# Interleaving two arrays: the first store as two DMAs of 8 KiB and 24 KiB rows

## The chip, the cores and the metric

The kernel runs on one core of a Trainium2 chip. The time is device time in microseconds (us) of one execution; several executions are compared by their median. The work is moved by the core's 16 DMA engines between the large memory (DRAM, where the inputs and the output lie) and the core's own memory of 128 partitions, and done by one computing engine, VectorE (DVE in the profile). DMAs are issued by two other engines: SyncE (SP) and ScalarE (ACT), each with a queue of its own.

## The reference

Two arrays of 32 x 256 x 1024 float32 values, x and y, are woven into one of twice the size: every even place of the result holds a value of x, every odd place one of y.

```python
result = np.zeros((batch, seq, dim * 2), dtype=np.float32)
result[..., 0::2] = x
result[..., 1::2] = y
```

Seen flat, the result is x[0], y[0], x[1], y[1] and so on. 33.5 MB of x and as much of y are read and 67.1 MB are written; there is no arithmetic.

## The kernel before, in words

The flat inputs are cut into 9 tiles. A tile has 128 rows, one for each partition, and the rows of a tile lie one behind the other in DRAM. Tiles 1 to 7 are W = 8192 values wide (rows of 32 KiB, 4 MiB for each of x and y), tile 0 and tile 8 have 4096 (rows of 16 KiB, 2 MiB). Two buffers each for x (`xt`), y (`yt`) and the woven output (`ot`) are used in turn.

A tile is woven in pieces of at most 4096 values per row: tile 0 is piece 0, tiles 1 to 7 give two pieces each (1 to 14), tile 8 is piece 15. A piece of 4096 columns of input makes 8192 columns of output, so each of the 16 stores moves 128 rows of 32 KiB, 4 MiB. Even pieces use the first output buffer, odd ones the second.

Three engines run in their own order, written out by hand:

- SP issues the loads (L52): x of tile 0, then x and y of tile 1, 2 and so on in turn. From tile 2 on it waits (L59, L62) until VectorE has woven the last piece of the tile two before, since the buffer is the same. y of tile 0 is issued by ACT instead. The first load of either queue is moved ahead of the program's opening.
- VectorE weaves a piece with two copies: L72 puts x at the even columns of the output buffer, L75 puts y at the odd ones. Ahead of them it waits for the loads (L68, L74) and, from piece 2 on, for the store that used the same output buffer before (L70).
- ACT waits until both copies of a piece are done (L78) and issues its store (L79).

A DMA adds 16 to its semaphore when it has landed. The stores of the even pieces count on one semaphore, those of the odd pieces on the other, and L70 waits for piece i until the semaphore of its parity has reached 16 times the number of earlier pieces of that parity: `16 * (i // 2)`. At the end ACT waits for all even stores (L83) and SP for all odd ones (L88), and the semaphores are set back.

Each DMA of 128 rows is spread over the 16 DMA engines, 8 rows to each.

Of the kernel before, what the change touches and what calls it, by code (L numbers as in the profile page):

```python
# [3 lines left out]


def _interleave(nc, x, y, out):
    P = 128
    W = 8192
    fp32 = mybir.dt.float32  # L10

    total = 1
    for s in x.shape:
        total *= s
    assert total % (P * W) == 0
    FIRST = 4096
    widths = [FIRST] + [W] * (total // (P * W) - 1) + [W - FIRST]
    n = len(widths)

    def flat(ap):  # L20
        return ap.rearrange("b s d -> (b s d)")

    fx, fy, fo = flat(x), flat(y), flat(out)
    at = [P * sum(widths[:k]) for k in range(n)]

    def rows(ap, k, scale=1):
        a, w = scale * at[k], scale * widths[k]
        return ap[a : a + P * w].rearrange("(p w) -> p w", p=P)

    xt = [nc.alloc_sbuf_tensor(f"xt{b}", [P, W], fp32).ap() for b in (0, 1)]  # L30
    yt = [nc.alloc_sbuf_tensor(f"yt{b}", [P, W], fp32).ap() for b in (0, 1)]
    ot = [nc.alloc_sbuf_tensor(f"ot{b}", [P, W], fp32).ap() for b in (0, 1)]

    xsem = [nc.alloc_semaphore(f"xsem{b}") for b in (0, 1)]
    ysem = [nc.alloc_semaphore(f"ysem{b}") for b in (0, 1)]
    woven = nc.alloc_semaphore("woven")

    pieces = []
    for k, w in enumerate(widths):
        step = w // 2 if w > W // 2 else w  # L40
        pieces += [(k, c, c + step) for c in range(0, w, step)]
    last = {}
    for i, (k, _, _) in enumerate(pieces):
        last[k] = i
    m = len(pieces)
    end = (m - 1) % 2
    osem = [None, None]
    for b in (1 - end, end):
        osem[b] = nc.alloc_semaphore(f"osem{b}")

    def load(eng, tile, ap, k, sem):
        return eng.dma_start(out=tile[:, : widths[k]], in_=rows(ap, k)).then_inc(sem, 16)  # L52

    load(nc.sync, xt[0], fx, 0, xsem[0])
    load(nc.scalar, yt[0], fy, 0, ysem[0])
    for k in range(1, n):
        b = k % 2
        if k >= 2:
            nc.sync.wait_ge(woven, 2 * last[k - 2] + 1)  # L59
        load(nc.sync, xt[b], fx, k, xsem[b])  # L60
        if k >= 2:
            nc.sync.wait_ge(woven, 2 * last[k - 2] + 2)  # L62
        load(nc.sync, yt[b], fy, k, ysem[b])

    for i, (k, a, e) in enumerate(pieces):
        b = k % 2
        if a == 0:
            nc.vector.wait_ge(xsem[b], 16 * (k // 2 + 1))  # L68
        if i >= 2:
            nc.vector.wait_ge(osem[i % 2], 16 * (i // 2))  # L70
        o = ot[i % 2][:, : 2 * (e - a)]
        nc.vector.tensor_copy(out=o[:, 0::2], in_=xt[b][:, a:e]).then_inc(woven, 1)  # L72
        if a == 0:
            nc.vector.wait_ge(ysem[b], 16 * (k // 2 + 1))  # L74
        nc.vector.tensor_copy(out=o[:, 1::2], in_=yt[b][:, a:e]).then_inc(woven, 1)  # L75

    for i, (k, a, e) in enumerate(pieces):
        nc.scalar.wait_ge(woven, 2 * i + 2)  # L78
        nc.scalar.dma_start(  # L79
            out=rows(fo, k, 2)[:, 2 * a : 2 * e], in_=ot[i % 2][:, : 2 * (e - a)]  # L80
        ).then_inc(osem[i % 2], 16)

    nc.scalar.wait_ge(osem[1 - end], 16 * (m // 2))  # L83
    used = sorted(s.num for s in [*xsem, *ysem, woven, osem[1 - end]])
    assert used == list(range(used[0], used[-1] + 1)), used
    nc.scalar.sem_clear(range(used[0], used[-1] + 1))
    turns = (m + 1) // 2
    nc.sync.nop(nofuse=True).wait_op(osem[end], 16 * turns, "sem-ge").then_inc(  # L88
        osem[end], -16 * turns
    )  # L90

def kernel(tc, x, y, out):
    nc = tc.nc
    tc.close()
    tc.compile()

    _interleave(nc, x, y, out)

    blocks = nc.main_func.blocks
    for engine in (mybir.EngineType.SP, mybir.EngineType.Activation):  # L100
        opening = blocks[0].instructions
        at, moved = next(
            (b, i)
            for b in blocks[1:]
            for i in b.instructions
            if i.engine == engine and i.opcode == "DMACopy"
        )
        assert not (moved.sync_info and moved.sync_info.on_wait)
        body = at.instructions
        body.remove(moved)  # L110
        gate = next(
            n
            for n, i in enumerate(opening)
            if i.engine == engine and i.opcode == "Drain"
        )
        opening.insert(gate, moved)
        at.instructions = body
        blocks[0].instructions = opening


# [1 line left out]
_INS = ['x', 'y']  # L122
_OUTS = [((32, 256, 2048), 'float32')]


# [23 lines left out]
```

## Time and profile before

| | us |
|---|---|
| three runs | 314.58, 315.33, 317.65 (median 315.33) |
| the profiled execution | 314.62 |
| its span, first to last instruction | 313.3 |
| VectorE busy | 72.6 (32 copies, 2.29 to 2.30 each) |
| VectorE waiting for stores at L72 | 159.4 (13 times) |
| VectorE waiting for y at L75 | 47.2 (8 times) |
| VectorE waiting for x at L72 | 20.7 (2 times) |

All times in the text count from the first instruction of the span unless it says otherwise. A line such as "L72 DVE COPY" names the line of the kernel, the engine and the operation. A DMA issue has two times: how long the issuing engine is held (0.33 to 0.43 us here for loads, 0.34 to 0.36 for stores) and how long it takes until the data has landed (29.1 us in the middle for a store, 43.7 for x and 60.9 for y of a full tile). The second contains the time in which the DMA stands in its queue behind others.

Some landings and issues of the first 90 us, from the trace:

| | issued | landed |
|---|---|---|
| x of tile 0, y of tile 0 | 0.00, 0.12 | 11.46, 13.30 |
| x of tile 1, y of tile 1 | 1.57, 1.95 | 25.16, 42.07 |
| x of tile 2, y of tile 2 | 13.81, 16.01 | 55.42, 74.76 |
| store 0 | 16.02 | 39.62 |
| store 1 | 44.42 | 67.50 |
| store 2 | 48.83 | 86.81 |

### The profile page before, as it was taken

What the parts mean: (1) busy time and instruction counts of PE and PEld (TensorE: products, weight loads), DVE (VectorE), ACT (ScalarE), POOL (GpSimd) and SP (SyncE); (2) the same over time, 40 slices, a digit from 0 to 9 for tenths busy, and PEclk for the clock granted to TensorE, in tenths of its full rate; (3) what the DMA queues carried; (4) which work ended last, traced back from release to release, by engine and by line L of the source; (5) the groups of instructions that cost most, each with busy time, mean ns of one, the idle gap of its engine ahead of it and who ended that gap; (6) DMA issues with size and microseconds to landing.
All of it is one profiled execution on the core that took longest, in us unless ns stands there. A gap on an engine that the chain in (4) does not pass through costs nothing.

```text
span 313.3 us, 114 instructions
## 1 busy us (share of the span) xinstructions
DVE 72.6 (23%) x32; POOL 0.2 (0%) x4
## 2 busy tenths in 40 slices
DVE  0502062022050220502205022040221402250320
POOL 0000000000000000000000000000000000000000
DMA  8999999999999999999999999999999999999998
GB/s 347 456 389 414 448 423 431 439 423 448 418 452 410 460 402 469 402 469 402 460 410 456 414 439 431 423 448 423 448 414 456 406 464 402 435 435 464 406 443 360
DMA packets 4896, 134.22 MB, mean 428 GB/s; under 512 B 544, under 2 KB 544, under 8 KB 544
## 3 DMA queue, kind: packets, MB, share of 16 engines
q10 hardware_dynamic: 2448, 69.21, 51.2%
q1 hardware_dynamic: 2448, 65.01, 48.6%
HBM read 67.11 MB, written 67.11 MB: 428 GB/s over the span
## 4 chain that ended last, share of the span: by engine, by line
DMA 73%; DVE 11%; another core or an unknown queue 10%; issue 0%; SPq 0%; DVEq 0%
DMA out_dram<-ot 61%; DMA yt<-in_y_dram 13%; DVE ot L75 6%; DVE ot L72 5%; SPq L52 0%; DVEq L70 0%
## 5 line engine op out<-in xcount | busy, mean ns | idle before, releaser
L72 DVE COPY ot<-xt 128x4096 f32<-128x4096 f32 x16 | 36.7, 2295 | 180.0 <-DMA out_dram<-ot 159.4
L75 DVE COPY ot<-yt 128x4096 f32<-128x4096 f32 x16 | 36.7, 2292 | 47.2 <-DMA yt<-in_y_dram 47.2
L133 POOL MEMSET const-bfloat16-1.0<- 128x1 bf16 x1 | 0.1, 101 | 0.0
L133 POOL MEMSET const-uint8-127<- 128x1 uint8 x1 | 0.1, 101 | 0.0
L133 POOL MEMSET const-float32-0.0<- 128x1 f32 x1 | 0.1, 98 | 0.2 <-issue 0.2
L133 POOL MEMSET const-float32-1.0<- 128x1 f32 x1 | 0.1, 98 | 0.0
## 6 DMA issues: line engine op xcount, KB each, us to landing
out_dram<-ot ACTq DMA_DIRECT2D x16, 4096.0 KB, 29.1
xt<-in_x_dram SPq DMA_DIRECT2D x7, 4096.0 KB, 43.7
yt<-in_y_dram SPq DMA_DIRECT2D x7, 4096.0 KB, 60.9
xt<-in_x_dram SPq DMA_DIRECT2D x2, 2048.0 KB, 25.2
yt<-in_y_dram ACTq DMA_DIRECT2D x1, 2048.0 KB, 13.2
yt<-in_y_dram SPq DMA_DIRECT2D x1, 2048.0 KB, 51.2
```

The costliest lines, as they stand in the source:

```text
L72: nc.vector.tensor_copy(out=o[:, 0::2], in_=xt[b][:, a:e]).then_inc(woven, 1)
L75: nc.vector.tensor_copy(out=o[:, 1::2], in_=yt[b][:, a:e]).then_inc(woven, 1)
L133: nc = _bacc.Bacc("TRN2", target_bir_lowering=False, num_devices=1)
```

## The change

The store of piece 0 is no longer one DMA but two, issued by ACT one behind the other. The first takes the first 2048 of the 8192 output columns of each row (128 rows of 8 KiB, 1 MiB), the second the other 6144 (128 rows of 24 KiB, 3 MiB). Both add 16 to the even semaphore, so every wait on that semaphore counts 16 more than before: piece 2 waits for 32, piece 4 for 48, and the closing wait for 144. The odd semaphore's numbers stay as they were. All other stores, all loads and all copies are unchanged.

```diff
+    def parts(i, w):
+        return [slice(0, w // 4), slice(w // 4, w)] if i == 0 else [slice(0, w)]
+
+    def stored(b, i):
+
+        return sum(16 * len(parts(j, W)) for j in range(b, i, 2))
...
         if i >= 2:
-            nc.vector.wait_ge(osem[i % 2], 16 * (i // 2))
+            nc.vector.wait_ge(osem[i % 2], stored(i % 2, i))
...
         nc.scalar.wait_ge(woven, 2 * i + 2)
-        nc.scalar.dma_start(
-            out=rows(fo, k, 2)[:, 2 * a : 2 * e], in_=ot[i % 2][:, : 2 * (e - a)]
-        ).then_inc(osem[i % 2], 16)
+        for c in parts(i, 2 * (e - a)):
+            nc.scalar.dma_start(
+                out=rows(fo, k, 2)[:, 2 * a : 2 * e][:, c], in_=ot[i % 2][:, c]
+            ).then_inc(osem[i % 2], 16)

-    nc.scalar.wait_ge(osem[1 - end], 16 * (m // 2))
+    nc.scalar.wait_ge(osem[1 - end], stored(1 - end, m))
...
-    turns = (m + 1) // 2
-    nc.sync.nop(nofuse=True).wait_op(osem[end], 16 * turns, "sem-ge").then_inc(
-        osem[end], -16 * turns
-    )
+    turns = stored(end, m)
+    nc.sync.nop(nofuse=True).wait_op(osem[end], turns, "sem-ge").then_inc(
+        osem[end], -turns
+    )
```

## The prediction

> **What bounds the kernel now.** I read the head of the page first, then the DMA busy time by stretches, then the chain and the waits. The kernel only moves data (section 3 of the page: 67.11 MB read, 67.11 MB written), so the first question is whether the 16 DMA engines ever rest. The page:
>
> ```profile
> span 313.3 us, 114 instructions
> ...
> DVE 72.6 (23%) x32; POOL 0.2 (0%) x4
> ...
> DMA  8999999999999999999999999999999999999998
> ...
> DMA packets 4896, 134.22 MB, mean 428 GB/s; under 512 B 544, under 2 KB 544, under 8 KB 544
> ...
> out_dram<-ot ACTq DMA_DIRECT2D x16, 4096.0 KB, 29.1
> ```
>
> The reader is to see that the only computing engine works 23% of the span while DMA is at 9 in all slices but the first and the last. Digits hide a per cent, so the second view is busy time by stretches (columns: stretch, its length, DVE, POOL, clock, DMA share, GB/s):
>
> ```profile
> 4.00:16.00 12.00, 4.50 (x2) 0.00 (x0) 1.00 1.01 434
> 16.00:44.00 28.00, 4.20 (x2) 0.00 (x0) 1.00 1.01 424
> 44.00:67.00 23.00, 4.79 (x3) 0.00 (x0) 1.00 1.01 435
> 67.00:106.00 39.00, 9.09 (x4) 0.00 (x0) 1.00 1.01 434
> 285.00:300.00 15.00, 4.59 (x2) 0.00 (x0) 1.00 1.01 437
> 300.00:312.00 12.00, 0.00 (x0) 0.00 (x0) 1.00 1.01 437
> ```
>
> From 4 to 67, the stretch that the change touches, and to the end, the share is 1.0: the engines are full, whether loads and stores alternate (67 to 106), loads run alone (part of 16 to 44) or a store runs alone (300 to 312). Now the chain:
>
> ```profile
> 1.95 40.12 DMA yt<-in_y_dram
> ...
> 44.42 23.08 DMA out_dram<-ot
> ...
> 297.53 2.30 DVE ot L75
> ```
>
> It looks as if the store of piece 1 (issued at 44.42) waits for y of tile 1 (landed at 42.07), and VectorE for stores (159.4 us in 13 waits by L79's view). But every DMA step of this chain is time in which the engines serve that transfer and its neighbour in turn; shortening a step only lengthens another.
>
> The trace's records of single packets give the unit. Each 32 KiB row is one packet of 1.213 us on one engine, each 16 KiB row 0.611 us, each semaphore packet 0.009 us. An engine has 8 rows of every DMA. Work of one engine: 14 loads and 16 stores of 32 KiB rows, 30 x 8 x 1.213 = 291.1; 4 loads of 16 KiB rows, 4 x 8 x 0.611 = 19.6; 34 semaphore packets, 0.3; together 311.0 us. The first packet starts at 1.02 and the last ends at 312.84, so 311.8 us hold 311.0 of work; 0.8 is the cold start (the first 16 KiB rows take up to 1.5 us). **So nothing in the order of transfers can win more than about 0.8 us, and a loss has to come from engines that rest or from rows that cost more.**
>
> **The change part by part.**
>
> *Bytes and rows.* Store 0, 8 x 1.213 = 9.70 us of each engine, becomes 8 rows of 8 KiB and 8 of 24 KiB. The trace has no stores of these sizes. The line through its two sizes (0.602 us per 16 KiB, 0.009 fixed) gives 0.310 and 0.912 us, together 1.222: +0.009 x 8 = +0.07, and one more semaphore packet +0.009. I take **+0.08 us**. Bounds: below, zero, since the same bytes move and 24 KiB lies between measured sizes; above, the instruction fetches in the same records, which are 8 KiB packets and took 0.474 to 0.549 us: 8 x (0.549 - 0.310) = +1.9 us for the small part. I stay by the line, as its rows are transfers of the same kind on the same queue, the fetches are not.
>
> *One more issue on ACT's queue.* L79 takes 0.34 us. It lies at 16.4, right behind the first, and ACT next has something to do when piece 1 is woven (44.4 before). Nothing; without that cover it would be 0.34.
>
> *What moves.* The packet records show how the engines share: where 16 KiB loads meet 32 KiB stores (268 to 276) each 4 us holds 1.22 us of loads and 2.79 of stores, so the two queues alternate row by row, whatever a row's size. A queue that sends smaller rows therefore gets less. Replay of one engine from 20.9 us, when store 0 sends its first row (issued 16.02): tile 1 still has 1 row of x and 8 of y to load.
> Before: store 0's 8 rows and 6 load rows alternate to 20.9 + 14 x 1.213 = 37.9 (landed 39.62); the last 3 rows of y run alone to 41.5 (landed 42.07). Then loads alone until store 1, issued 44.42, sends from about 48.7. Between 20.9 and 48.7 this makes 15 load rows.
> After: eight 8 KiB rows alternate with eight load rows, one 24 KiB row, and the ninth: 20.9 + 8 x 0.310 + 9 x 1.213 + 0.912 = 35.2. So **y of tile 1 lands near 35.8 rather than 42.07**, and store 1 is issued near 38.1 rather than 44.42. The other seven 24 KiB rows alternate with five more load rows to 20.9 + 2.48 + 8 x 0.912 + 14 x 1.213 = 47.7, so **store 0 lands near 49.3 rather than 39.62**. Store 1 is queued by then and starts after one or two load rows, near 49 to 50: 15 or 16 load rows since 20.9, where before there were 15. The hole that store 1 left in its queue (37.9 to 48.7) goes, but loads filled that hole, so its going wins no time.
>
> *The wait that grows.* VectorE's wait before piece 2 (L70) now asks for both halves of store 0: its copies begin near 49.3, not at 44.31. Behind it are piece 2's two copies, behind these the loads of tile 3 (issued 46.62 and 48.82, now near 51.6 and 53.9) and store 2 (48.83, now 53.9). Who is late? The load queue reaches tile 3 at 75.1, when y of tile 2 is through: 23 us of cover. Store 2 sends at 67.9, behind store 1: 14 us of cover, and it takes the place of store 1's rows at once. Both costs are zero here.
>
> *Steady state and end.* From store 1 on every row is as before, with the loads level or one row (1.2 us) further ahead of the stores. The slack of this state is 9.7 us: a store is issued at 77.11, the one in front of it lands at 86.81. At the end y of tile 8 lands at 297.50, store 15 is issued at 299.86 and sends at 302.7 to 303.2, just as store 14 runs out (last packet 303.16). Loads further ahead make this place safer, by up to about 1 us. The closing waits change only in the number for the even semaphore.
>
> Sum: +0.08 us on the profiled execution, 314.62 (its span 313.3 and 1.3 around it), so 314.7. The three runs have the median 315.33, 0.7 above that execution, lowest 314.58. On the median: 315.33 + 0.08 = **315.4 us**.
>
> **The rivals.**
>
> *A fixed price for the second DMA.* If the engines paused between two DMAs, the price would be what passes from a store's last packet to its landing: 38.0 to 39.62, 1.6 us. Then 315.33 + 1.6 = 316.9, still within 1%. Against it: store 15's packets follow store 14's with no gap, share 1.01. Chance 0.05.
> The Trainium skill, "DMA: Bandwidth & Descriptors", section "Anatomy of one DMA", fits a DMA as about 2.0 us fixed plus bytes over 436 GB/s (for the path through gpsimd, which this kernel doesn't use); by it, as an estimate, the second DMA costs 2.0 us, 317.3. The trace agrees with the slope (437 GB/s) but shows the fixed part beside other packets.
>
> *Rows of the new sizes are dear; slower.* Place: store 0's 256 rows. If 24 KiB is sent as three of 8 KiB and each costs what an instruction fetch cost, an engine spends 32 x 0.549 = 17.6 us instead of 9.7: +7.9, 323.2. It decides (1%, 3.15 us) from (9.70 + 3.15) / 32 = 0.40 us per 8 KiB. For it: no record of a 24 KiB row. Against: 16 KiB rows cost half of 32 KiB to within 1%, so a row of 8 KiB would have to leave the line by 0.09. Chance 0.06.
>
> *A hole at the end; slower.* If the stores came out ahead by n load rows instead, y of tile 8 would land about 1.8 n later (a 16 KiB and a 32 KiB row each) and store 15 find its queue empty, with half a microsecond of slack: n = 2 gives +3, 318.4. The replay gives the other sign. Chance 0.02.
>
> *Faster.* The 0.8 us of cold start is before the changed place. Below 1% in any case; 0.03 for what runs scatter (314.58 to 317.65).
>
> *The split doesn't act* (the two DMAs share the engines as one): the time is the same, 315.4; it is part of the forecast's share.
>
> **How the numbers follow.** Forecast 0.84; 1% (3.15 us) is about what a measurement of this kernel tells from no change. Within 1%: 0.84 + 0.05 = 0.89; slower: 0.06 + 0.02 = 0.08; faster 0.03. The range: below, 314.4, the lowest run less 0.2 for the slack at the end; above, 317.4, which takes in the +1.9 us bound of 8 KiB rows and the fixed price.
>
> **What would show it.** Packets 5040 (4896 + 128 + 16) with 134.22 MB; an issue more; y of tile 1 landing near 36, VectorE's copy of it there and then a wait for store 0 of some 11 us to near 49; store 1 issued near 38; from 67 on the old rhythm of 38.7 us per tile; DMA share 1.0 in 16 to 67. Wrong if: share below 1 in 16 to 67 (a pause or dear rows), y of tile 1 still near 42 (no row-by-row turns), or packets at the end with no store behind store 14.

## The result and the profile after

Over 22 runs of each the changed kernel took 314.63 us (median; 314.23 to 315.27), the kernel before 315.81 (314.42 to 318.88). The ratio of the averages (314.64 and 316.24) is 0.9949, 95% interval 0.9925 to 0.9973. That is half a per cent faster in the average and 0.4% in the median, where 315.4 and no change had been forecast. The lowest times hardly differ (314.23 and 314.42); what went away is the upper part of the scatter. In a later comparison the changed kernel was at 314.80 (314.23 to 315.15) against 315.55 (314.45 to 319.59), ratio 0.9972 (0.9948 to 0.9996). Slow runs, more than 1.5% above the fastest of the same kernel, count in the medians and spans given here but not in the ratios.

The profiled executions show nothing of this gain: 314.58 us after, 314.62 before. The page of the changed kernel, the lines that answer to those of before:

```profile
span 313.2 us, 115 instructions
...
DMA  9999999999999999999999999999999999999998
...
DMA packets 5040, 134.22 MB, mean 428 GB/s; under 512 B 560, under 2 KB 560, under 8 KB 560
...
out_dram<-ot ACTq DMA_DIRECT2D x15, 4096.0 KB, 32.7
...
out_dram<-ot ACTq DMA_DIRECT2D x1, 3072.0 KB, 33.9
...
out_dram<-ot ACTq DMA_DIRECT2D x1, 1024.0 KB, 17.2
```

The same bytes go in 144 more packets, the engines are as full as they were, and the stores wait longer in their queue (32.7 us from issue to landing, 29.1 before). The same by stretches (stretch, its length, DVE, POOL, clock, DMA share, GB/s):

```profile
4.00:16.00 12.00, 4.38 (x2) 0.00 (x0) 1.00 1.01 433
16.00:44.00 28.00, 4.70 (x3) 0.00 (x0) 1.00 1.01 421
44.00:67.00 23.00, 4.50 (x2) 0.00 (x0) 1.00 1.02 440
67.00:106.00 39.00, 9.09 (x4) 0.00 (x0) 1.00 1.00 433
285.00:300.00 15.00, 4.59 (x2) 0.00 (x0) 1.00 0.99 426
300.00:312.00 12.00, 0.00 (x0) 0.00 (x0) 1.00 1.01 437
```

The chain of the changed kernel's first 55 us no longer runs through y of tile 1 but through the second part of store 0, which VectorE now waits for:

```profile
16.54 33.91 DMA out_dram<-ot
...
50.47 2.30 DVE ot L79
```

So the order of the transfers changed as foreseen, and the profiled time did not. The gain has to be looked for in executions that neither profile shows. The question for the runs was what makes some executions of the kernel before longer than 314.6.

### The profile page after: what moved, and what is told of

Read it like the earlier page. It is cut to its first block, busy times and chain, and to the rows that moved or that the text cites. A ratio compares the mean times of both kernels' runs of the same rounds, so it can differ in the third digit from the quotient of the medians.

```text
span 313.2 us, 115 instructions
## 1 busy us (share of the span) xinstructions
DVE 72.7 (23%) x32; POOL 0.2 (0%) x4
## 4 chain that ended last, share of the span: by engine, by line
DMA 84%; DVE 11%; ACTq 0%; issue 0%
DMA out_dram<-ot 65%; DMA yt<-in_y_dram 15%; DVE ot L82 6%; DVE ot L79 5%; DMA xt<-in_x_dram 4%; ACTq L87 0%
## 6 DMA issues: line engine op xcount, KB each, us to landing
out_dram<-ot ACTq DMA_DIRECT2D x15, 4096.0 KB, 32.7
out_dram<-ot ACTq DMA_DIRECT2D x1, 1024.0 KB, 17.2
```

## The experiments

A view that turned out to carry the answer is worked out from the trace's landing records. Every DMA is counted by 16 increments, one for each engine that moved 8 of its rows. The **lag** of a DMA is the time of its last increment less the median of its 16. The Trainium skill, "DMA: Bandwidth & Descriptors", section "Why a DMA increments its semaphore by 16 and not by 1", says that only the full count means that all data has landed; the traces agree, since every wait here ends with the last of the 16.

### Where a long execution loses its time

First theories: "lead" (loads too little ahead of the stores, so that the end gets a hole) against "gap" (the stretch without stores, 38 to 48.7 us). Two more executions of the kernel before, unchanged:

> The kernel before, unchanged, profiled once more, to see an execution of it that took longer than the one shown (314.62; the median of 22 runs is 315.81, the highest 318.88). Theory 'lead' (the loads stand too little ahead of the stores, so that in some executions y of tile 8 lands late and store 15 finds store 14 already gone): a long execution shows engines at rest just before store 15, between about 300 and 305 us, and y of tile 8 landing later than 297.5. Rival 'gap' (the stretch in which store 1's queue is empty and loads run alone, 38 to 48.7 us, is at times slower): a long execution shows x and y of tile 2 and everything after them late by the same amount, already at 60 us, and no rest at the end. If this execution is near 314.6 it tells nothing.

> As before_a: the same kernel, another execution. Lead: any excess over 314.6 us stands as rest of the DMA engines ahead of store 15. Gap: any excess is there by 60 us.

Measured: 315.49 us (before_a) and 314.90 (before_b). Later two more were taken, before_c and before_d:

> The kernel before once more, to see an execution above 316.5 us if one comes. Theory: its excess is that of one DMA engine, which falls behind during store 0 (and perhaps further later), while the other 15 end near 312.6. Rival: all 16 engines end later together.

> As before_c: another execution of the kernel before; one engine behind from store 0 on with the others at 312.6, or, by the rival, all of them late.

Measured: 314.61 and 316.02. The longest of them at its end (same columns as above):

```profile
300.00:312.00 12.00, 0.00 (x0) 0.00 (x0) 1.00 1.01 437
312.00:314.00 2.00, 0.00 (x0) 0.00 (x0) 1.00 0.00 0
```

for the execution of 314.62, and for that of 316.02:

```profile
300.00:312.00 12.00, 1.28 (x1) 0.00 (x0) 1.00 1.01 437
312.00:314.00 2.00, 0.00 (x0) 0.00 (x0) 1.00 0.04 16
```

There is no hole before 312 (share 1.01, 437 GB/s in both). But after 312 the longer execution still has a share of 0.04. A packet counts where it starts, so this is one more row on one engine (1.213 of 16 x 2 us). The packet records say it outright: 15 of its engines end between 312.27 and 312.74, and one at 314.33. The lags, in us:

```
execution (kernel before)       x1    s0    y1    s1    y2   ...  y8    s15    time   time - lag of s15
first profile                  0.22  0.20  0.19  0.20  0.19      0.23  0.26  314.62  314.36
before_c                       0.41  0.39  0.41  0.40  0.43      0.36  0.33  314.61  314.28
before_b                       0.31  1.90  0.67  1.11  0.67      0.69  0.61  314.90  314.29
before_a                       0.16  2.53  1.31  0.17  2.49      2.51  1.26  315.49  314.23
before_d                       0.31  2.52  1.34  0.28  2.65      3.11  1.89  316.02  314.13
```

(x1 is x of tile 1, s0 is store 0, and so on.) Until x of tile 1 has landed all 16 engines are together. With store 0, in the three longer executions, one engine falls behind and never catches up: every engine has 8 rows of every DMA, all of them are busy all the time, and so a loss stays until the end. While two queues alternate, a row lost shows twice in the landings (2.5), at the end once (1.26). **The time of an execution is 314.25, give or take 0.12, plus the lag of its last store** (314.25, the time without a lag, is called the floor below). For these executions both first theories fall: no rest at the end, and what is late at 60 us is one engine. The rival of before_c, all engines late together, falls too.

Where the engine falls behind can be seen in the packets. Store 0 is issued at 16.02 us and its first row is recorded at 20.67. Just ahead of that, from 17.2 us on, load packets take longer than their 1.213 us in every execution, 14 to 15 us in sum over the engines, some 0.9 us for each on average. This is the join of store 0 to the running load, called the hold-up below. In before_a and before_d one packet at 18.7 took 1.9 us longer; in the first profile the longest excess was 0.89. The sum is no larger in the long executions (14.8 and 14.4) than in the short ones (14.3 and 14.8): what differs is how unevenly the engines share it. Y of tile 2 is issued in the same moment (16.01), but it is not the likely cause, as the issues of other loads (13.81, 46.62, 48.82) hold no packet. In before_d the loss also grew later: 1.34 at y of tile 1, 1.89 at the end.

### Lead alone, and the end

The kernel before with store 1 issued one copy later (delay_s1; `idle` is a scratch tile, DELAY is 2048):

```diff
...
+        if i == 1:
+            nc.vector.tensor_copy(out=idle[:, :DELAY], in_=yt[b][:, a : a + DELAY])
         nc.vector.tensor_copy(out=o[:, 1::2], in_=yt[b][:, a:e]).then_inc(woven, 1)
```

> The kernel before with one more copy of 2048 columns (about 1.1 us, into a scratch tile) on VectorE ahead of the y copy of piece 1, so that store 1 is issued about 1.1 us later: the loads run alone for one row more and stand one row further ahead of the stores for the rest, as in the changed kernel, while the empty stretch of the store queue gets longer (about 12 us, not 11). Lead: the median falls to that of the changed kernel, 314.6 to 314.9, highest under 316, ratio to before about 0.995. Gap: no faster than before, ratio 1.000 to 1.004.

Measured: 315.06 (314.53 to 315.88, 12 runs), before on the same chip 314.65 (314.50 to 317.43), ratio 0.9997 (0.9981 to 1.0012). Store 1 landed at 69.59, as late as in the changed kernel (69.75), so the lead was there. Its profiled execution (315.08) has a load packet that took 1.9 us longer at 18.6, and an engine that lags by 1.99 at store 0 and 0.76 at the end. So with the lead alone an engine still falls behind. Whether the lead limits how far, this run can't say: the median of the kernel before was near the floor in this comparison and could hardly fall, 1 of 12 runs lies above 315.6 beside 5 of 23, and a lag of 0.76 also occurs in the cut kernels below.

The kernel before with the last piece's y copy and store in two halves (early_s15; the loop over the two stores and the waits, which count one more, are left out here):

```diff
...
+            nc.vector.tensor_copy(out=o[:, 1 : 2 * h : 2], in_=yt[b][:, a : a + h]).then_inc(woven, 1)
+            nc.vector.tensor_copy(out=o[:, 2 * h + 1 :: 2], in_=yt[b][:, a + h : e]).then_inc(woven, 1)
```

> The kernel before with the last y copy in two halves and store 15 as two DMAs of 16 KiB rows, the first issued as soon as the first half is woven: store 15's first row can go 1.1 us earlier after y of tile 8 has landed; nothing ahead of that is changed. Lead: the long executions lose up to 1.1 us, median 315.81 less 0.5 to 1.1, ratio 0.996 to 0.999, and the scatter shrinks. Gap: the place is not touched, ratio 1.000 within 0.002 and the same scatter (highest near 318).

Measured: 315.21 (314.56 to 316.79, 12 runs, 4 of them above 315.6), ratio 1.0002 (0.9979 to 1.0026): the scatter of before. Making store 15 earlier is worth nothing, so the end is not the place. Its profiled execution (316.24) again has the lag from store 0 (2.07) on, growing from 0.82 at y of tile 1 to 1.96 at y of tile 8. Here two engines are behind: near 18.5 us two packets took 1.3 us longer, and at the end two engines stop at 314.41 and 314.54, the others by 313.18. Between 67 and 291 us single load and store packets of 0.03 to 0.4 us excess add up to 3.7 us. This growth is a second source of long executions, seen in this one and in before_d.

### The cut of store 0

The changed kernel again (after_b), and with its parts exchanged (rev_24_8):

```diff
-        return [slice(0, w // 4), slice(w // 4, w)] if i == 0 else [slice(0, w)]
+        return [slice(0, 3 * w // 4), slice(3 * w // 4, w)] if i == 0 else [slice(0, w)]
```

> The changed kernel, unchanged, beside the kernel before on the chip of the next run. New theory 'start' (the executions of the kernel before that take longer do so because one of the 16 DMA engines is held up by 1 to 4 us when store 0 joins the running load of x of tile 1, near 18 us; an engine's rows are fixed, so it stays behind to the end; the 8 KiB rows make that hold-up shorter for the worst engine): load packets between 9 and 25 us are longer than 1.213 us by 7 to 8 us in sum over the engines and by at most 0.7 us each (0.61 in the first profile), the engines' last packets end within 0.6 us of each other, highest time under 315.4, median 314.3 to 314.8. Rival 'lead' (what counts is that loads stand a row further ahead): the same times, but no statement on the early packets.

> The changed kernel with its two parts exchanged: store 0 goes out as 24 KiB rows first, then 8 KiB rows. The same number of rows, the same waits, store 1 queued behind store 0 as in the changed kernel, the same row or so of lead; y of tile 1 lands near 38 to 40. Start: what decides is the row that the store begins with, and this is nearly the old one, so the hold-up near 18 us is as before: 11 to 15 us in sum, single packets longer by 0.8 to 2, engines' ends up to 1 us apart or more, highest time 316 or more, ratio to before 0.998 to 1.002, slower than the changed kernel by 0.1 to 0.4%. Lead, or a filled store queue: as the changed kernel, median and scatter (314.6, highest under 315.4).

Measured: 314.80 (314.23 to 315.15) and 314.81 (314.38 to 315.53); before beside them 315.55 (314.45 to 319.59). In the changed kernel the hold-up is split: 7.6 to 8.3 us in sum near 18 us and 3.2 to 6.2 more near 32, when the second part begins; with 24 KiB first it stays at 11.8 near 18 us, as expected. But the time is the same, so theory "start", that 8 KiB rows in front are what helps, falls.

Two equal parts (half_16_16), and store 0 cut by partitions instead of columns (rows64; the waits on the even semaphore count 16 more):

```diff
-        return [slice(0, w // 4), slice(w // 4, w)] if i == 0 else [slice(0, w)]
+        return [slice(0, w // 2), slice(w // 2, w)] if i == 0 else [slice(0, w)]
```

> The changed kernel with store 0 in two equal parts, 128 rows of 16 KiB each. The profiles so far show that a longer execution of the kernel before has one DMA engine that loses 0.6 to 1.3 us while store 0 is on its way (its landing of store 0 is 2 to 2.5 us behind the middle engine, that of y of tile 1 0.7 to 1.3), and stays behind to the end; with store 0 in two column parts none did. Theory 'unequal rows' (store 0's rows of 32 KiB beside load rows of 32 KiB hold one engine; shorter rows don't): as the changed kernel, no engine behind by over 0.5 us at y of tile 1, median 314.4 to 314.9, highest under 315.6. Rival 'two DMAs' gives the same here and differs in the next run.

```diff
...
+        for c in [slice(0, P // 2), slice(P // 2, P)] if i == 0 else [slice(0, P)]:
             nc.scalar.dma_start(
-                out=rows(fo, k, 2)[:, 2 * a : 2 * e], in_=ot[i % 2][:, : 2 * (e - a)]
+                out=rows(fo, k, 2)[c, 2 * a : 2 * e], in_=ot[i % 2][c, : 2 * (e - a)]
...
```

> The kernel before with store 0 as two DMAs by partitions, 64 rows of 32 KiB each (every engine 4 rows of each): two DMAs and one wait more, but rows of 32 KiB as before, so turns, lead and the empty store queue from 38 to 48.7 us are as before (y of tile 1 lands near 42). Unequal rows, and also the rivals lead and filled queue: the scatter of the kernel before (several of 12 times above 315.6, an engine behind at store 0), ratio 0.998 to 1.002. Two DMAs as such: narrow as the changed kernel, highest under 315.6.

Measured: 16 and 16 KiB 314.74 (314.39 to 315.07), as the changed kernel; the kernel before beside it had a median of 314.67 but went up to 318.92, ratio 0.9980 (0.9953 to 1.0007). By partitions 321.15 (318.83 to 333.43, 6 runs), ratio 1.0142 (1.0078 to 1.0206): nothing that any theory had expected. Its profiled execution, by stretches:

```profile
16.00:44.00 28.00, 2.30 (x1) 0.00 (x0) 1.00 1.01 393
...
300.00:312.00 12.00, 4.18 (x2) 0.00 (x0) 1.00 0.82 352
312.00:320.00 8.00, 0.00 (x0) 0.00 (x0) 1.00 0.65 279
```

Between 25 and 60 us load and store packets lose 40 us in sum (0 in the kernel before), the lag is 3.59 at x of tile 2 and grows to 10.13 at y of tile 8, and then there is the hole that the prediction had as a rival: store 15 was issued at 307.33, too late for the engines that had finished store 14, and the share from 300 to 312 falls to 0.82. (After 312 it is low also because 15 of the engines are through by 318.4, and one only at 320.34.) So two DMAs are no help by themselves when the cut is by partitions. More this run can't say, because with 64 partitions an engine may also read other partitions than for the loads and the other stores. (The Trainium skill, "DMA: Bandwidth & Descriptors", section "The descriptor swizzle", gives the engines' partitions for 128 only; what it is for 64 no run here shows.)

### Rows of the store, or of the load

The kernel before, store 0 whole, but x and y of tile 1 each loaded by two DMAs of 16 KiB rows (loads_split; the waits for tiles loaded so count 16 more); and store 0 cut 30 and 2 KiB (big_first):

```diff
...
+        for c in [slice(0, W // 2), slice(W // 2, W)] if k == 1 else [slice(0, widths[k])]:
+            eng.dma_start(out=tile[:, c], in_=rows(ap, k)[:, c]).then_inc(sem, 16)
```

> The kernel before with store 0 whole (32 KiB rows), but the loads of x and y of tile 1, which it meets, each as two DMAs of 16 KiB rows. Store 0 then ends near 35.5 us and y of tile 1 lands near 42 as before; lead and empty store queue are as before. Theory 'row quantum' (when store 0 joins the load, one engine's load packet is held for one whole store row more than the others': 1.21 us with 32 KiB rows, less with shorter store rows; what the loads' rows are doesn't matter): scatter as before, several of 12 times 0.6 us or more over the lowest, some above 315.6. Rival 'equal rows' (the hold comes only where store rows and load rows have the same length): narrow, none above 315.3.

```diff
-        return [slice(0, w // 4), slice(w // 4, w)] if i == 0 else [slice(0, w)]
+        return [slice(0, 15 * w // 16), slice(15 * w // 16, w)] if i == 0 else [slice(0, w)]
```

> The changed kernel with store 0 cut 30 KiB and 2 KiB (the long rows first). Two DMAs, unequal rows, 8 turns more, store 1 queued behind store 0, as in the changed kernel. Row quantum: the first store rows are nearly the old ones, so an engine can lose 1.14 us: times in two groups about 1.1 us apart, the upper at 315.3 to 316. Rivals equal rows, two DMAs, or the filled store queue: narrow, as with 16 and 16 KiB (314.4 to 315.1).

Measured: with the loads split 315.04, and all 12 runs between 314.98 and 315.16, beside 314.38 to 316.33 for the kernel before; ratio 0.9994 (0.9980 to 1.0008). y of tile 1 lands at 42.51, the store queue is empty from 36 until store 1, and still the profiled execution (314.99) has no engine that has lost time: the lag is 0.3 at every load from y of tile 1 on and 0.31 at store 15. (Stores 1 to 11 do show a lag of 1.0, most of a row, of which 0.3 is left at the end. So the lag of a store alone, while two queues alternate, need not be a loss.) The filled queue is therefore not needed, and neither is more lead: the median engine lands y of tile 8 0.3 us later than in the kernel before, not earlier. What this costs is a longer hold-up for all: 19.2 us in sum near 18 us, 0.3 more per engine than the 14.3 of the kernel before. By stretches (last column GB/s), first the kernel before, then the one with split loads:

```profile
16.00:20.00 4.00, 0.00 (x0) 0.00 (x0) 1.00 1.13 393
```

```profile
16.00:20.00 4.00, 0.00 (x0) 0.00 (x0) 1.00 0.98 332
```

The 393 GB/s of these 4 us fall to 332, and the floor of this kernel is higher: 314.99 less the lag of 0.31 is 314.68, so 314.25 doesn't hold for it.

With 30 and 2 KiB: 314.88 (six runs 314.49 to 314.60, six 315.15 to 315.49), ratio 0.9993 (0.9980 to 1.0005). Two groups came, but about 0.7 us apart by their medians, not 1.1, and none as high as 315.6; nor are they as narrow as the rivals had it. Row quantum already falls with the split loads, which it had expected to scatter. Then single executions, of 24 and 8 KiB (rev_b, rev_c), 30 and 2 KiB (big_first_b, big_first_c), and the changed kernel (after_c), and store 0 in four parts of 8 KiB (quad8):

> The kernel with 24 KiB rows first, a second execution: its 12 times fell into two groups, 314.4 to 314.6 and 315.0 to 315.5. Row quantum: an execution of the upper group has one engine that lost about 0.9 us (one 24 KiB row) at store 0, one of the lower group none. Rival: in the upper group all engines end later together.

> As rev_b, a third execution: one engine behind by about 0.9 us from store 0 on if it is of the upper group, none if it is of the lower.

> The kernel with 30 and 2 KiB rows, another execution. Its 12 times fell into two groups, 314.49 to 314.60 and 315.15 to 315.49; the profiled one was of the lower and had no engine behind. Theory: an execution of the upper group has one engine behind from store 0 on, by 0.6 to 0.9 us at the end, and no growth afterwards. Rival: all engines end later together.

> As big_first_b, a third execution: if near 315.2, one engine behind by 0.6 to 0.9 us from store 0 on and the others at 312.5.

> The changed kernel, a third execution. Its 34 times lie between 314.23 and 315.27. If this one is above 314.8: one engine behind by 0.3 to 0.7 us, or all engines later by as much because the two joins (near 18 and 32 us) held all of them longer. If it is below 314.5: no engine behind.

```diff
-        return [slice(0, w // 4), slice(w // 4, w)] if i == 0 else [slice(0, w)]
+        return [slice(j * w // 4, (j + 1) * w // 4) for j in range(4)] if i == 0 else [slice(0, w)]
```

> Store 0 as four DMAs of 8 KiB rows each. If the length of store 0's rows sets what an engine can lose, this is at least as narrow as the changed kernel (highest under 315.3). The loads get 32 turns beside store 0 rather than 16, so they stand further ahead of the stores (y of tile 1 again near 36, store 0 landing some 20 us later, near 70) and store 15 is safer; median 314.3 to 314.8. If the further lead turns against the kernel (store 15 then waits for store 13 rather than for y of tile 8), 315 to 318.

Measured: rev_b 314.46 and rev_c 314.44, both of the lower group and without an engine behind (lags 0.24 to 0.32 from tile 1 on); big_first_c 314.49, also without. The upper group was caught in big_first_b, 315.22:

```
execution                      x1    s0 (1st part)  y1    y8    s15    time   time - lag of s15
30 + 2 KiB, big_first_b       0.31   2.19          0.89  0.29  0.94  315.22  314.28
8 + 24 KiB, after_c           0.38   1.06          0.24  0.23  0.81  314.98  314.17
8 + 24 KiB, first profile     0.30   1.49          0.31  0.41  0.25  314.58  314.33
8 + 24 KiB, after_b           0.23   0.21          0.16  0.13  0.14  314.28  314.14
16 + 16 KiB                   0.26   0.23          0.23  0.22  0.21  314.54  314.33
```

So an engine falls behind in the cut kernels too, in some executions; the rule, time = 314.25 plus lag, holds for them, but the lags at the end that were seen stay under 1 us. The third row shows again that a lag of stores (1.2 to 1.3 at stores 1 to 11) can be gone at the end: only that of store 15 goes into the time. Four parts of 8 KiB gave 314.69 (314.20 to 315.56; before beside it 315.71, 314.49 to 319.41), ratio 0.9977 (0.9951 to 1.0003), with six runs under 314.5 and five from 315.13 on. Store 0 was complete at 61.28, not near 70, and y of tile 1 at 35.16. The times are no narrower than with one cut, which speaks against a loss whose size goes by the length of the store's rows; but only an execution without a lag was profiled (314.37, lag 0.16), so what the five upper runs lose was not seen.

### What is shown and what stays open

Of 125 runs of the kernel before in all comparisons 44 took over 315.6 us (up to 319.59), between 4 and 11 in each of the six; of 82 runs of the five column cuts none did (up to 315.56), nor of the 12 with split loads. How often the long runs come differs: the median of the kernel before lay between 314.65 and 315.81, and where it was 314.65 or 314.67 there was nothing to win in the median.

Shown, for executions up to 316.24 us: the excess is the lag of one engine (of two in early_s15), and it begins when store 0 joins the load of tile 1. Shown by the runs: cutting store 0 by columns, or that load, bounds the times. Not needed for this are 8 KiB rows in front (24 + 8, 16 + 16), a filled store queue or more lead (loads_split). What a row more of lead alone would do is open (delay_s1); two DMAs cut by partitions (rows64) made it worse. All six kernels that stay narrow have rows of store 0 that differ in length from the rows they meet, but in the cuts a smaller lag is left, so unequal rows are the likeliest reason and no more.

Why one engine loses the extra time stays open. Open is also what the longest executions lose: none above 316.24 was profiled, yet 10 of the 22 runs of the kernel before in the first comparison are longer than that, and most of the difference of the averages lies in them. They may have a larger lag, or a hole at the end as rows64 had. No version was clearly better than the changed kernel.

## Why the prediction was wrong, point by point

- **The price of the edit was right.** 8 KiB packets took 0.309 us and 24 KiB packets 0.912 (forecast 0.310 and 0.912); the profiled span is 313.2 for 313.3. The bound of +1.9 us and the rival of dear rows are out.
- **The replay was right.** y of tile 1 landed at 36.52 (forecast 35.8), store 1 was issued at 38.87 (38.1), store 0 was complete at 50.45, in a second execution 49.06 (49.3), tile 3's loads were issued at 52.79 and 54.99 (51.6 and 53.9). From there the rhythm is 38.72 us per tile (y of tile 3 at 112.16, of tile 4 at 150.88). y of tile 8 landed at 296.26, 1.24 earlier than before, as "one row further ahead" had it.
- **The fixed price for a second DMA is zero here:** 314.58 against 314.62, where the rival had +1.6 and the page of the Trainium skill, "DMA: Bandwidth & Descriptors", by its section "Anatomy of one DMA", some +2.0 as an estimate. The trace doesn't agree with that as a price of time where other packets fill the engines.
- **The step that failed** is the last of the sum, "On the median: 315.33 + 0.08". It took the one profiled execution as the kernel, and the 0.7 us to the median as scatter that the change would leave alone. "Nothing in the order of transfers can win more than about 0.8 us" fits that execution, which had no engine behind (lag 0.26). It is not true of the median one: at 315.81 it carries, by the rule above, about 1.5 us of one engine's lag. The executions on either side, 315.49 and 316.02, had 1.26 and 1.89. The mechanism was missing from the list of rivals; "faster" got 0.03 "for what runs scatter". The three times shown, 314.58, 315.33 and 317.65, were the sign: scatter of 3 us upward over a profile near the very bottom says that the profile doesn't stand for the usual run.
- **A term was put in the wrong place.** The 0.8 us were called cold start, which lies "before the changed place". The same trace holds the join's 14.3 us in sum, 0.9 for each engine, and that is at the changed place. The packets of the first 9 us add 8.9 us in sum, under 0.6 for each on average. Together this is 1.5 us, more than the 0.8 that the sum left over, because the sum took 1.213 us for a row: the steady rhythm, 38.72 us for the 32 rows of a tile, makes it 1.210, some 0.7 us less over 240 rows. In the changed kernel the hold-up is 11.4 to 13.8 us in sum, so its smaller size wins at most 0.2 us; what counted is how unevenly it is shared.
- **Luck:** 314.63 lies inside the stated range (from 314.4), but its lower end allowed 0.2 us for the slack at the end, and early_s15 shows that making the end earlier wins nothing.
- **The rival of a hole at the end** did not come true in the changed kernel (share 1.01 from 300 to 312). In rows64 there is such a hole (share 0.82), brought about by one engine's lag of 10 us, not by the order of the queues.

## What to carry to other kernels

In a kernel that keeps all 16 DMA engines full, compare the profiled execution with the median and the highest run before using its sum: if it lies at the bottom, the typical run loses time that the profile doesn't have. Look at the 16 landings of each DMA, not only the last. No other engine took over the rows of the one that was behind: in before_d it worked on alone to 314.33 when the other 15 were through by 312.74. So a loss stays, and while no engine rests the time is a floor plus the lag of the last store. The place to look first was where the second queue joined the running one for the first time; a later join, that of store 1, held no packet.

## What the runs showed of the hardware that was not expected

- When the first store joins a running load, the load packets of all engines are held, 14 to 15 us in sum (0.9 each) for 32 KiB rows on both sides; one engine can lose 1.9 us in a single packet (before_a, before_d, delay_s1). When store 1 joins at 48.5 us in the kernel before, no packet is held.
- With the loads of tile 1 in 16 KiB rows the time is almost fixed: 12 runs within 0.18 us, though the hold-up is larger (19.2 us in sum).
- Two DMAs of 64 partitions instead of one of 128, once in a kernel, made it longer: 321.15 us in the median of six runs against 314.67, ratio 1.0142 (1.0078 to 1.0206).
